# The attention of a diffusion layer in an order written out for all engines, with two sets of ring slots

## The chip, the cores and the metric

One core of a Trainium2 chip runs the whole layer. The metric is the device time of one execution in microseconds (us); the kernel is run several times and the median counts. One more execution is recorded by the hardware profiler, and the rows below are from that one.

The core has five engines that run their own queues in order: PE (TensorE, matrix products into PSUM), VectorE (DVE in the profile), ScalarE (ACT), GpSimd (POOL) and the sync engine (SP), which here only issues DMA transfers. Semaphores carry the waits between them.

## The reference, cut to what matters

```python
def reference(x, c, ctx, c_ctx, w_ada, b_ada, ...):        # 256 latent tokens, 256 context tokens, width 1024
    mod = jnp.split((silu_c @ w_ada[l] + b_ada[l])[:, None, :], 6, axis=-1)      # six rows of 1024
    h = modulate(rms_norm(x, g_mix_pre[l]), mod[0], mod[1])
    y, yc = token_mixing(h, hc, w_in[l], sink[l], g_q_a[l], w_uq[l], g_kv_a[l], w_ukv[l], w_o[l], ...)
    x = x + mod[2] * rms_norm(y, g_mix_post[l])
    h2 = modulate(rms_norm(x, g_ffn_pre[l]), mod[3], mod[4])
    f = moe_ffn(h2, w_router[l], b_router[l], w_gate_up[l], b_gate_up[l], w_down[l], b_down[l])
    return x + mod[5] * rms_norm(f, g_ffn_post[l])

def token_mixing(h, hc, w_in, ...):
    qa, ka, va, cq, ckv, kr = jnp.split(h @ w_in, PROJ_SPLITS, axis=-1)
    out_a = windowed_gqa(qa, ka, va, ka_c, va_c, sink)       # 8 heads, 2 of keys and values, with a sink logit
    qn, qr, kn, vb = mla_project(cq, ckv, g_q_a, w_uq, g_kv_a, w_ukv)   # low rank 384 and 256, norm, up-projection
    out_b = mla_latent(qn, qr, kn, kr, vb, kn_c, kr_c, vb_c)            # 8 heads of 64 + 32
    y = jnp.concatenate([out_a, out_b], axis=-1) @ w_o
```

The mixture of experts takes the best 4 of 32 experts for each token; every expert has 12 MiB of weights (gate and up 8, down 4), so 384 MiB in all, and nearly all of the transferred bytes.

## The kernel before

Everything is float32. The work stands in this order:

1. *Run-up.* The first two rows of the modulation (products of `w_ada` on PE), norm, transposes and the combined input projection `w_in`, each weight split into a high and a low part (`split`, L127) so that three products (`mm3`, L134) give full precision. `stage_a` and `stage_b` apply rope and transpose q and k of the GQA heads; `lowrank` (L354) norms and transposes the MLA latents; `up` (L461) makes the MLA keys `pk`.
2. *Attention.* 16 heads in 8 pairs `u`: 0 to 3 GQA, 4 to 7 MLA. For a pair: `weights(u)` (L636) makes scores with transposed keys on PE, ScalarE takes the exponential into `pT`; the probabilities are summed over keys in `pa` (one head on VectorE, one on GpSimd, L670); `values(u)` (L675) multiplies by v and by ones, then VectorE takes the reciprocal `rz` and writes `oT`; `mix(u)` (L693) multiplies by the output projection into the PSUM tiles `y`. The softmax needs row maxima first: `top_a(j)` for GQA, `top_b(h)` for MLA heads (reductions on VectorE), and `shift(g)` transposes them. The MLA tensors come from `k_up(i)` (L497: copies on ScalarE into `k96`, eight transposes, splits), `q_up(n, t)` (L511: product, copy and rope into `q96`, four transposes, split) and `v_up(i)`.
3. *The other four rows of the modulation* ("ada", chunks 0 to 3) are made beside all this, away from PE. Item i = 4 ch + s is one load of 1 MiB (`ada_load`, L404) and its work (`ada_do`, L415): two halves, each multiplied by a column of silu(c) and summed into `accs[ch]`. A half listed in `ADA_G` goes through ScalarE (product, L422) and GpSimd (sum, L423); the other half is one VectorE instruction (L425). Both write the same sum, so they come one after the other. `column` and `spread1` bring finished rows into the form that the layer needs; `spread0` loads a gain row for it on ScalarE's queue.
4. *Router* (`XSEQ`, L66 and L903), then 32 *experts* (L1094): for each, `G_` (gate and up, matmuls at L972 into `pw`), `T_` (SwiGLU), `D_` (down), `scatter` into `acc`.

Expert weights come in 384 loads of 1 MiB (`load`, L703). Load number n goes to slot `RSEQ[n % 18]`: `d0` to `d2` are the tiles that held the latents and the GQA q and k, `r` a ring slot, `k0 q0 b0 k1 q1 b1` the MLA tensors of head group 0 and 1, `x` four slots in the work memory of the attention, free after the last `values` and `mix`. The ring (`slot`, L79) has R1 = 5 slots of 1 MiB that everything uses: ada items, pieces of `w_in`, `w_ukv`, `w_uq`, the split of v (`v_split`), `w_o` (`load_wo`), gain rows, `scr` and `ar_` in the run-up.

Order: the sync engine always follows the program text, and an issue that waits for its slot holds the ones behind it. In the run-up the other engines are ordered by the compiler's scheduler. From L725 on PE follows the text too; ScalarE, VectorE and GpSimd follow it only from L787, after `mix(6)`. Whatever the order is, it is fixed before the run.

Of the kernel before, what the change touches and what calls it, by code (L numbers as in the profile page):

```python
# [18 lines left out]
P = 128  # L19
# [51 lines left out]
def layer_kernel(ctx, tc, x, cx, cc, wadr, bada, grows, win0, winB, winC, winD, wuqa, wuqb, wukv, wo, wr, wexp, bgu, bgx, bdn, cols, rows, consts, out):  # L71
# [6 lines left out]

    def slot():  # L79
        return ring.tile([P, 2048], F32, name="slot", tag="slot")  # L80

# [112 lines left out]
    def load_ada(i):  # L194
        w = slot().rearrange("p (k c) -> p k c", c=D)
        nc.sync.dma_start(w, wadr[i].rearrange("p (k c) -> p k c", c=D))
        return w
# [7 lines left out]
    scr = slot().rearrange("p (j d) -> p j d", j=2)  # L205
# [19 lines left out]
    def fetch(src, n):  # L225
        w = slot()
        nc.sync.dma_start(w[:, 0:n], src)
        return w
# [61 lines left out]
    ar_ = slot().rearrange("p (j d) -> p j d", j=2)  # L290
# [150 lines left out]
    fkv = fetch(wukv, 1024)  # L441
    fuq = [fetch(wuqa, 1536)]
# [5 lines left out]
    fuq += [fetch(wuqb, 1792)]  # L448
# [48 lines left out]
    def k_up(i):  # L497
        k96 = pqa.tile([P, 8, 96], F32, name="k96", tag="ct", bufs=2)
        S.copy(k96[:, :, 64:96], krt[:, i][:, None].to_broadcast([P, 8, 32]))
        S.copy(k96[:, :, 0:64], pk[i].rearrange("p (h d) -> p h d", h=8))  # L500
        for g in range(2):
            pt = ptp((96, 4, P))
            for j in range(4):
                PE.transpose(pt[:, j], k96[:, g * 4 + j], ident)
            ks = slice(i * P, (i + 1) * P)
            split(kTm[0][g][0:96, :, ks], kTm[1][g][0:96, :, ks], pt)
# [4 lines left out]
    def q_up(n, t):  # L511
        if n == 0:
            q96[t] = pqa.tile([P, 8, 96], F32, name="q96", tag="ct", bufs=2)
# [3 lines left out]
        S.copy(q96[t][:, n * 4:n * 4 + 4, 0:64], pq_[:, :, 0:64])  # L517
        rope(sm, q96[t][:, n * 4:n * 4 + 4, 64:96].rearrange("p h (a d) -> p h a d", a=2),
             pq_[:, :, 64:96].rearrange("p h (a d) -> p h a d", a=2), row[:, t, R_CB:R_CB + 32],
             row[:, t, R_SB:R_SB + 32], 16, 4)  # L520
        pt = ptp((96, 4, P))
        for j in range(4):
            PE.transpose(pt[:, j], q96[t][:, n * 4 + j], ident)
# [23 lines left out]
    def load_wo(i):  # L547
        w = slot()
# [11 lines left out]
    def spread0(ch):  # L560
        gs_[ch] = slot()
        S.dma_start(gs_[ch][:, 0:D], bass.AP(tensor=grows.tensor, offset=grows.offset + (0 if ch == 0 else 1) * D,
# [31 lines left out]
    def top_a(j):  # L594

        for t in range(NT):
            s_ = [pmm((P, 512)) for h in range(2)]
            kb = 3 - t
            for h in range(2):
                PE.matmul(s_[h][:, kb * P:(kb + 1) * P], ident_b, mask_b[:, t * P:(t + 1) * P], start=True, stop=False,  # L600
                          skip_group_check=True)
            for h in range(2):
                PE.matmul(s_[h], qTg[0][HALF[h], t, j], kTg[0][HALF[h]], start=False, stop=True, skip_group_check=True)
            for h in range(2):
                V.tensor_reduce(mxs["a"][:, t, 64 * h + j:64 * h + j + 1], s_[h], axis=AX.X, op=ALU.max)
# [30 lines left out]
    def weights(u):  # L636
# [3 lines left out]
        pa_[u] = [av.tile([P, 2, T], F32, name="pa", bufs=3) for h in range(2)]  # L640
        for g in range(2):
# [26 lines left out]
            for h in range(2):  # L668
                S.activation(pT_[u][h][:, 2 * g:2 * g + 2], st[h], AF.Exp, scale=A_SCALE if a else B_SCALE)  # L669
        for h in range(2):  # L670
# [4 lines left out]
    def values(u):  # L675
        pT, pa = pT_.pop(u), pa_.pop(u)
# [26 lines left out]
    def load(e, js):  # L703
        for j in js:
            q = RSEQ[len(slots) % len(RSEQ)]
            if q == "r":
                w = slot()
# [20 lines left out]
    k_up(1)  # L728
    top_a(1)
    ada(1)  # L730
    k_up(2)
    k_up(3)
    top_a(2)
    top_a(3)
    v_split()
    ada(2)
    for t in range(NT):
        q_up(0, t)
    for i in range(2):
        v_up(i)  # L740
    shift("a")
    clear(1)
    for t in range(NT):
        q_up(1, t)
    for i in range(2, 4):
        v_up(i)
    open_y()
    ada(1)
    load_wo(0)
    for j in range(4):  # L750
        weights(j)
        if j:
            values(j - 1)
        top_b(2 * j)
        top_b(2 * j + 1)
        if j > 1:
            mix(j - 2)
        if j % 2:
            shift(j // 2)
        if j == 0:  # L760
            load_wo(1)
            spread0(0)
        if j == 1:
            column(1)
            spread1(0)
        ada(2)
        if j == 3:
            load(0, range(0, 3))
    for u in range(4, 8):
        weights(u)  # L770
        values(u - 1)
        mix(u - 2)
        if u < 6:
            load_wo(u - 2)
        if u == 4:
            column(2)
            ada(2)
        if u == 5:
            load(0, range(3, 6))
        if u == 6:  # L780
            spread0(3)
            spread1(3)
    values(7)
    mix(6)
    if MANX:
        stM.close()
# [520 lines left out]
```

## Time and profile before

| | us |
|---|---|
| median of 3 runs | 1241.83 |
| lowest, highest | 1241.19, 1244.47 |
| the profiled execution | 1246.29 |
| its span, first to last instruction | 1244.5 |
| PE busy | 1125.8 |
| VectorE, ScalarE, GpSimd busy | 309.8, 241.7, 131.0 |
| bytes read from HBM | 444.6 MB |

The busy times are sums over stages that have different limits. The useful way to read this profile is by stage: how fast DMA runs, and which wait ends last in each.

### The profile page before, as it was taken

The numbers are of one execution on the slowest core, as the hardware profiler recorded it, in microseconds if no ns is written. First come the engines' busy times: TensorE is split into PE (matmuls) and PEld (weight loads), VectorE is DVE, ScalarE is ACT, GpSimd is POOL, SyncE is SP. The second block draws the span as 40 slices with busy tenths as digits, with TensorE's granted clock in tenths as the row PEclk, the third lists the DMA queues.
The fourth block names the chain that finished last, engine by engine and source line by source line (L and its number), as shares of the span: only waits on it lengthen the run. The fifth ranks groups of instructions, "written<-read, shape, count | busy, mean of one in ns | idle before, by whom it ended". The sixth has DMA issues, their size and how long they took to land.

```text
span 1244.5 us, 13660 instructions
## 1 busy us (share of the span) xinstructions
PE 1125.8 (90%) x5455; PEld 485.7 (39%) x5455; DVE 309.8 (25%) x657; ACT 241.7 (19%) x518; POOL 131.0 (11%) x177
## 2 busy tenths in 40 slices
PE   7796758999999999999999999989898989898985
PEld 1694435656334343433323232323232323232321
DVE  3878472335211111111111111111111111111112
ACT  3645220213111111111111111111111111111201
POOL 0414030111000101011010101010101010101000
PEclk9897876999899999999999999999999999999998
DMA  9654150558989999999999999999999999999994
GB/s 366 253 213 172 65 220 1 225 233 320 421 323 421 420 420 420 420 420 419 421 421 420 420 419 421 421 420 421 420 421 421 420 421 420 421 420 421 420 421 197
DMA packets 63195, 446.60 MB, mean 359 GB/s; under 512 B 7284, under 2 KB 7540, under 8 KB 10008
## 3 DMA queue, kind: packets, MB, share of 16 engines
q1 hardware_dynamic: 62648, 444.24, 87.0%
q10 hardware_dynamic: 480, 1.44, 0.4%
q8 instruction: 45, 0.74, 0.2%
q14 instruction: 22, 0.18, 0.0%
HBM read 444.60 MB, written 1.05 MB: 358 GB/s over the span
## 4 chain that ended last, share of the span: by engine, by line
DMA 53%; PE 36%; DVE 7%; issue 2%; ACT 1%; POOL 0%; SPq 0%; POOLq 0%; ACTq 0%; DVEq 0%
DMA slot<-in_wexp 51%; PE pw L972 18%; PE y L696 3%; DMA slot<-in_wadr 2%; PE px L939 2%; PE mm L660 2%; PE acc L1002 1%; PE mm L267 1%; DVE accw L425 1%; PE mm L681 1%; PE pf L985 1%; PE pr L516 1%; PE mm L138 1%; PE mm L139 1%; PE mm L137 1%
## 5 line engine op out<-in xcount | busy, mean ns | idle before, releaser
L972 PE MATMUL pw<-slot,xg 128*64 128x512 f32 x2048 | 468.5, 599 | 19.3 <-DMA slot<-in_wexp 19.3
L972 PE MATMUL pw<-slot,actT 128*64 128x512 f32 x1024 | 242.8, 600 | 28.6 <-DMA slot<-in_wexp 27.1
L972 PEld LDWEIGHTS pw<-slot,xg 128*64 128x64 f32 x2048 | 136.6, 137 | 302.9 <-issue 232.0
L990 DVE TENSOR_TENSOR z<-pf,bg 128x512 f32<-128x512 f32 x64 | 44.3, 692 | 755.5 <-PE pf L985 755.5
L972 PEld LDWEIGHTS pw<-slot,actT 128*64 128x64 f32 x1024 | 68.6, 136 | 179.1 <-issue 101.7
L994 ACT ACTIVATE sg<-z 128x256 f32<-128x256 f32 x64 | 26.7, 417 | 311.9 <-DVE z L992 311.9
L979 ACT COPY gu<-pw 128x512 f32<-128x512 f32 x64 | 37.5, 586 | 230.2 <-PE pw L972 230.2
L939 PEld LDWEIGHTS px<-oh,xt 128*128 128x128 f32 x480 | 57.5, 196 | 23.9 <-issue 23.9
L1002 PE MATMUL acc<-y,ctt 64*128 64x512 f32 x256 | 63.6, 615 | 0.7 <-ACT y L979 0.7
L939 PE MATMUL px<-oh,xt 128*128 128x128 f32 x480 | 63.2, 286 | 0.3 <-DVE cnt L1057 0.3
L951 ACT ACTIVATE xg<-px,vcol 128x128 f32<-128x128 f32 x120 | 45.2, 457 | 92.2 <-PE px L939 92.2
L985 PEld LDWEIGHTS pf<-con,gu 128*128 128x128 f32 x256 | 26.8, 140 | 52.7 <-issue 51.1
L985 PE MATMUL pf<-con,gu 128*128 128x128 f32 x256 | 42.0, 286 | 0.7 <-ACT gu L979 0.7
L979 ACT COPY y<-pw 128x512 f32<-128x512 f32 x32 | 18.8, 587 | 91.1 <-PE pw L972 91.1
L929 POOL TENSOR_SCALAR oh<-con,posm,r 128x64 f32<-128x64 f32 x60 | 33.9, 581 | 2.5 <-DVE posm L869 2.5
L696 PE MATMUL y<-slot,of 128*128 128x512 f32 x64 | 33.7, 678 | 0.0
L996 DVE TENSOR_TENSOR sg<-z,sg 128x256 f32<-128x256 f32 x64 | 27.2, 425 | 18.0 <-ACT sg L994 18.0
L1002 PEld LDWEIGHTS acc<-y,ctt 64*128 64x128 f32 x256 | 22.0, 186 | 21.8 <-issue 18.4
L669 ACT ACTIVATE pT<-mm 128x512 f32<-128x512 f32 x32 | 17.2, 594 | 61.8 <-PE mm L660 58.8
L997 DVE SCALAR_TENSOR_TENSOR actT<-z,sg 128x256 f32<-128x256 f32 x64 | 27.2, 425 | 2.2
L267 PE MATMUL mm<-slot,siluz 128*4 128x512 f32 x40 | 19.4, 635 | 7.4 <-DMA slot<-in_wadr 7.4
L966 ACT COPY ctt<-px 128x256 f32<-128x256 f32 x32 | 12.0, 375 | 61.8 <-PE px L965 61.8
(450 smaller groups left out, 920.4 us busy)
## 6 DMA issues: line engine op xcount, KB each, us to landing
slot<-in_wexp SPq DMA_DIRECT2D x384, 1024.0 KB, 19.9
slot<-in_wadr SPq DMA_DIRECT2D x20, 1024.0 KB, 5.6
ax<-in_wadr SPq DMA_DIRECT2D x4, 1024.0 KB, 4.9
slot<-in_wo SPq DMA_DIRECT2D x4, 1024.0 KB, 7.7
slot<-in_win SPq DMA_DIRECT2D x2, 1024.0 KB, 8.1
slot<-in_winD SPq DMA_DIRECT2D x2, 768.0 KB, 7.3
slot<-in_winB SPq DMA_DIRECT2D x2, 576.0 KB, 5.6
ct<-in_cx SPq DMA_DIRECT2D x2, 512.0 KB, 13.2
```

The costliest lines, as they stand in the source:

```text
L267: PE.matmul(pad[ch][n], siluz[:, 2 * s + k], w[:, k, n * 512:(n + 1) * 512], start=(s == 0 and k == 0), stop=(last and k == 1), skip_group ...
L696: PE.matmul(y[t][n], oT[k][:, t * P:(t + 1) * P], wov[k][:, n * 512:(n + 1) * 512], start=(k == 0), stop=(k == KD - 1), skip_group_check=True)
L929: eng.tensor_scalar(oh[t][:, i], iota[:, 0:CAP], pos_ap(t), r2[t], op0=ALU.is_equal, op1=ALU.mult)
L939: PE.matmul(px[:, k, 0:ne * CAP], xt[t][:, kk * P:(kk + 1) * P], self.oh[t][:, 0:ne].rearrange("p e c -> p (e c)"), start=(k == 0 and t == ...
L951: S.activation(o, i, AF.Identity, scale=vcol[:, 1, kk:kk + 1], bias=vcol[:, 0, kk:kk + 1])
L972: PE.matmul(pt[HALF[h]], lhs(k), wk(k, h), start=(k == 0), stop=(k == KD - 1), skip_group_check=True)
L979: S.copy(y, pt)
L985: PE.transpose(pf[:, b].rearrange("p h c -> p (h c)"), gu[:, b * P:(b + 1) * P], ident)
L990: V.tensor_tensor(z, pf, bias[:, :, :, None].to_broadcast([P, 4, 2, CAP]), op=ALU.add)
L996: V.tensor_tensor(sg, zg, sg, op=ALU.mult)
L997: V.scalar_tensor_tensor(actT[:, 4 * c:4 * c + 4], zl, 1.0, sg, op0=ALU.add, op1=ALU.mult)
L1002: PE.matmul(acc[t][n], ctt[HALF[n], t], y[HALF[n]], start=False, stop=last, skip_group_check=True)
```

## The change

The tags and sizes: the ring is cut into three `slot` tiles and two `wide` ones. Loads of the run-up alternate between them (`any_slot`); `w_ukv`, both `w_uq` pieces and `w_o` take `wide` ones, ada items of the attention and `v_split` the three others. `scr` and `ar_` move to held tiles, the gain rows to the tag `ct`, which `k96` and `q96` use too. `q96` becomes one tile for each half. In the expert loads two `r` become `w`.

The work on engines: chunk 3 of the ada sums also goes half through ScalarE and GpSimd (twelve items instead of eight). The subtraction in `v_split` goes from VectorE to GpSimd. The sums `pa` move from the end of `weights` to the start of `values` (`adds`). In `q_up` rope comes ahead of the copy.

The order: from the first `ada_load` of the attention on, ScalarE, VectorE and GpSimd follow the text as well. `k_up` and `q_up` are cut into a part that computes (`k_mid`, `q_up`) and one that transposes (`k_flip`, `q_flip`), and the text is a list of calls: key transposes among the GQA maxima, then `weights(0)` to `weights(3)` with q and v up-projections between them, the expert loads `d0` to `d2`, then MLA maxima between `mix` calls, and MLA pairs. One ada item at a time stands between them, sixteen in all by `mix(5)`; then five loads of expert 0 and one of expert 1 follow, ahead of `weights(7)`.

```diff
-R1 = 5
+R1 = 3
-RSEQ = ("d0", "d1", "d2", "r", "r", "r", "k0", "q0", "b0", "k1", "q1", "b1", "r", "r", "x", "x", "x", "x")
-ADA_G = {(c, s, k) for c in (1, 2) for s in range(4) for k in range(1)}
+RSEQ = ("d0", "d1", "d2", "r", "r", "r", "k0", "q0", "b0", "k1", "q1", "b1", "w", "w", "x", "x", "x", "x")
+ADA_G = {(c, s, 0) for c in (1, 2, 3) for s in range(4)}
+    def wide():
+        return ring.tile([P, 2048], F32, name="slot", tag="wide", bufs=2)
+    def any_slot():
+        turn[0] += 1
+        return wide() if turn[0] % 5 in (3, 4) else slot()
-    scr = slot().rearrange("p (j d) -> p j d", j=2)
+    scr = held(1).rearrange("p (j d) -> p j d", j=2)
-    ar_ = slot().rearrange("p (j d) -> p j d", j=2)
+    ar_ = held(2).rearrange("p (j d) -> p j d", j=2)
-    fkv = fetch(wukv, 1024)
-    fuq = [fetch(wuqa, 1536)]
+    fkv = fetch(wukv, 1024, wide)
+    fuq = [fetch(wuqa, 1536, wide)]
-    fuq += [fetch(wuqb, 1792)]
+    fuq += [fetch(wuqb, 1792, wide)]
-        split(r[:, 0:1024], r[:, 1024:2048], fuq[1][:, 768:1792])
+        split(r[:, 0:1024], r[:, 1024:2048], fuq[1][:, 768:1792], eng=G)
-        w = slot()
+        w = wide()
         nc.sync.dma_start(w, wo[i])
-        gs_[ch] = slot()
+        gs_[ch] = pqa.tile([P, D], F32, name="gs", tag="ct", bufs=2)
     def values(u):
+        adds(u)
         pT, pa = pT_.pop(u), pa_.pop(u)
+    stM.close()
+    stM.enter_context(tc.manual_schedule(engines={SP, *[getattr(mybir.EngineType, e_) for e_ in MANX]}))
     ada_load()
     ada_load()
-    stM.close()
-    stM.enter_context(tc.manual_schedule(engines={SP, mybir.EngineType.PE}))
-    k_up(0)
-    top_a(0)
...
     v_split()
+    k_mid(2)
+    k_mid(3)
+    for i in (2, 3):
+        top_a(i - 2, 0)
+        k_flip(i)
+        top_a(i - 2, 1)
...
+    v_up(0)
+    q_up(0, 0)
+    v_up(1)
     shift("a")
     clear(1)
+    weights(0)
+    q_flip(0, 0)
+    q_up(0, 1)
+    v_up(2)
+    ada(1)
+    weights(1)
+    v_up(3)
+    q_flip(0, 1)
+    q_up(1, 0)
+    values(0)
+    ada(1)
+    weights(2)
+    q_flip(1, 0)
+    q_up(1, 1)
+    values(1)
+    ada(1)
+    load_wo(0)
+    weights(3)
+    q_flip(1, 1)
+    values(2)
+    load_wo(1)
+    load(0, range(0, 3))
     open_y()
     ada(1)
+    top_b(0)
+    mix(0)
+    spread0(0)
+    top_b(1)
+    top_b(2)
+    ada(1)
+    column(1)
+    top_b(3)
+    mix(1)
+    values(3)
+    ada(1)
+    load_wo(2)
+    top_b(4)
+    shift(0)
+    mix(2)
+    ada(1)
+    weights(4)
+    spread1(0)
+    top_b(5)
+    mix(3)
+    ada(1)
+    load_wo(3)
+    weights(5)
+    top_b(6)
+    values(4)
+    column(2)
+    top_b(7)
+    mix(4)
+    ada(2)
+    shift(1)
+    spread0(3)
+    values(5)
+    ada(1)
+    weights(6)
+    ada(1)
+    mix(5)
+    load(0, range(3, 8))
+    load(1, range(0, 1))
+    weights(7)
+    values(6)
+    spread1(3)
+    mix(6)
     values(7)
     mix(KD - 1)
-    load(0, range(6, 8))
-    load(1, range(0, 4))
+    load(1, range(1, 4))
     load(0, range(8, 12))
```

## Rows read from the trace of the kernel before

**Rows 1.** The page's 40 slices: busy share of the DMA engines, in tenths.

```profile
DMA  9654150558989999999999999999999999999994
```

**Rows 2.** Chain that ended last, whole span: start us, length us, what.

```profile
299.88 10.45 PE pw L972 x48
...
588.02 19.86 DMA slot<-in_wexp
...
1209.06 19.50 DMA slot<-in_wexp
```

**Rows 3.** Table of stages: busy us (instructions) by engine, granted clock, DMA share, GB/s.

```profile
155.00:186.00 31.00, 17.45 (x118) 11.50 (x116) 21.56 (x22) 7.58 (x12) 10.15 (x6) 0.76 0.61 228
186.00:217.00 31.00, 25.71 (x130) 17.30 (x132) 9.89 (x17) 2.54 (x5) 1.99 (x2) 0.64 0.00 1
249.00:280.00 31.00, 29.69 (x158) 18.01 (x157) 10.65 (x14) 4.34 (x8) 4.00 (x4) 1.00 0.58 231
300.00:588.00 288.00, 285.57 (x1364) 108.73 (x1361) 48.89 (x133) 48.39 (x110) 23.01 (x40) 0.98 0.98 405
588.00:1228.00 640.00, 591.84 (x2764) 210.19 (x2764) 87.58 (x215) 92.43 (x208) 43.76 (x76) 1.00 1.01 419
```

**Rows 4.** Timeline of the sync engine: start us, length us, line, operation, count.

```profile
268.16 1.28 SPq L713 DMA_DIRECT2D slot<-in_wexp  x3
...
284.35 17.76 SPq L713 DMA_DIRECT2D slot<-in_wexp  x6
```

**Rows 5.** Chain that ended last, end of the run-up and first key transposes.

```profile
94.26 1.21 DVE accw L425
...
110.06 0.61 DVE cn L359
...
117.71 1.89 PE tp L504 x8
```

**Rows 6.** The same chain in the attention: PE pieces at full clock.

```profile
138.47 1.95 PE pr L516 x6
...
216.09 1.62 PE mm L660 x22
...
230.17 3.79 PE mm L660 x32
233.97 1.88 PE mm L681 x16
...
236.71 3.63 PE y L696 x8
...
261.59 1.72 PE mm L570 x4
```

**Rows 7.** The same chain: waits, ada work, and PE pieces at half clock.

```profile
151.51 6.42 DMA slot<-in_wadr
157.95 1.16 ACT slot L422
159.18 2.37 POOL accw L423
...
172.57 5.28 DMA slot<-in_wadr
...
196.50 3.57 PE mm L570 x4
...
209.86 6.24 PE y L696 x8
...
265.68 0.60 ACT pT L669
```

**Rows 8.** Timeline of VectorE: the low part of the v split.

```profile
96.57 2.50 DVE L129 TENSOR_TENSOR slot<-slot 128x1024 fp32r<-128x1024 f32 x1 [0.92 <-ACT slot L128]
```

**Rows 9.** Line 672, VectorE's part: ns min/median/max, first and last start us.

```profile
L672 DVE TENSOR_TENSOR pa<-pT x8: 684/814/2330, 165.0 to 271.4; 128x512 f32<-128x512 f32 x8
```

**Rows 10.** Waits of the sync engine: us in total, times, longest.

```profile
SPq L713 <- PE mm L666: 40.0, 1, 40.0
```

More of the change, by code (lines that the diff above doesn't have):

```diff
@@ L194, in load_ada @@
     def load_ada(i):
-        w = slot().rearrange("p (k c) -> p k c", c=D)
+        w = any_slot().rearrange("p (k c) -> p k c", c=D)
         nc.sync.dma_start(w, wadr[i].rearrange("p (k c) -> p k c", c=D))
@@ L223, in norm_t, with fetch @@
             S.copy(xraw[2 * w + g][:, :, j], p_)
-    def fetch(src, n):
-        w = slot()
+    def fetch(src, n, get=any_slot):
+        w = get()
         nc.sync.dma_start(w[:, 0:n], src)
@@ L495, in layer_kernel, with k_mid, k_flip @@
                           mask_b[64 * c:64 * c + 64].rearrange("p (t k) -> p t k", t=NT))
[L497 to L500, printed above, removed]
+    k96 = {}
+    def k_mid(i):
+        k96[i] = pqa.tile([P, 8, 96], F32, name="k96", tag="ct", bufs=2)
+        S.copy(k96[i][:, :, 0:64], pk[i].rearrange("p (h d) -> p h d", h=8))
+        S.copy(k96[i][:, :, 64:96], krt[:, i][:, None].to_broadcast([P, 8, 32]))
+    def k_flip(i):
         for g in range(2):
@@ L511, in q_up @@
     def q_up(n, t):
-        if n == 0:
-            q96[t] = pqa.tile([P, 8, 96], F32, name="q96", tag="ct", bufs=2)
+        q96[n, t] = pqa.tile([P, 4, 96], F32, name="q96", tag="ct", bufs=2)
         pq_ = prow((P, 4, 96))
@@ L547, in load_wo @@
     def load_wo(i):
-        w = slot()
+        w = wide()
         nc.sync.dma_start(w, wo[i])
@@ L592, in layer_kernel, with top_a @@
     ess = {}
[L594 to L605, printed above, removed]
+    def top_a(j, t):
+        s_ = [pmm((P, 512)) for h in range(2)]
+        kb = 3 - t
+        for h in range(2):
+            PE.matmul(s_[h][:, kb * P:(kb + 1) * P], ident_b, mask_b[:, t * P:(t + 1) * P], start=True, stop=False,
+                      skip_group_check=True)
+        for h in range(2):
+            PE.matmul(s_[h], qTg[0][HALF[h], t, j], kTg[0][HALF[h]], start=False, stop=True, skip_group_check=True)
+        for h in range(2):
+            V.tensor_reduce(mxs["a"][:, t, 64 * h + j:64 * h + j + 1], s_[h], axis=AX.X, op=ALU.max)
     def top_b(h):
@@ L639, in weights @@
         pT_[u] = [av.tile([P, 4, T], F32, name="pT", bufs=4) for h in range(2)]
-        pa_[u] = [av.tile([P, 2, T], F32, name="pa", bufs=3) for h in range(2)]
         for g in range(2):
@@ L669, in weights, with adds @@
                 S.activation(pT_[u][h][:, 2 * g:2 * g + 2], st[h], AF.Exp, scale=A_SCALE if a else B_SCALE)
+    def adds(u):
+        pa_[u] = [av.tile([P, 2, T], F32, name="pa", bufs=3) for h in range(2)]
         for h in range(2):
@@ L705, in load @@
             q = RSEQ[len(slots) % len(RSEQ)]
-            if q == "r":
-                w = slot()
+            if q in "rw":
+                w = slot() if q == "r" else wide()
             elif q == "x":
@@ L741, in layer_kernel @@
+    k_mid(2)
[4 more added lines that the diff above has]
+        top_a(i - 2, 1)
+    k_mid(0)
+    k_mid(1)
+    for i in (0, 1):
+        top_a(i + 2, 0)
+        k_flip(i)
+        top_a(i + 2, 1)
+    v_up(0)
+    q_up(0, 0)
+    v_up(1)
     shift("a")
     clear(1)
[L743 to L746, printed above, removed]
+    weights(0)
[5 more added lines that the diff above has]
+    v_up(3)
@@ L747, in layer_kernel @@
+    q_flip(0, 1)
[13 more added lines that the diff above has]
+    load(0, range(0, 3))
     open_y()
     ada(1)
[L749 to L782, printed above, removed]
+    top_b(0)
[11 more added lines that the diff above has]
+    top_b(4)
@@ L783, in layer_kernel @@
+    shift(0)
[21 more added lines that the diff above has]
+    mix(5)
+    assert ada_n[0] == 16 and not ada_q
+    load(0, range(3, 8))
[4 more added lines that the diff above has]
+    mix(6)
     values(7)
-    mix(6)
-    if MANX:
-        stM.close()
-        stM.enter_context(tc.manual_schedule(engines={SP, *[getattr(mybir.EngineType, e_) for e_ in MANX]}))
```

24 lines of the change are left out of this document (7 added, 17 removed).

## The prediction, made before the changed kernel was run

> **What bounds the kernel now.** I read the page's slices first, then the chain that ended last, then the queue of the sync engine (SP), and only then the attention. The slices, 31 us each, say that the kernel has two parts: ten slices with low and middle digits of DMA, and then nines up to the end [rows 1]. In the chain that ended last, matmuls of the experts start at 299.88, and from 588.02 the chain is nothing but landings of expert weights of 19.9 us each, thirty-two of them, the last at 1209.06 [rows 2]. The table of stages confirms it: 419 GB/s from 588 on, with PE busy 592 of 640 us; between 300 and 588 it is the other way round, PE 285.6 of 288 us and DMA 405 GB/s [rows 3]. So the end is a stream of expert weights, 384 loads of 1 MiB. At 419 GB/s one takes 1.0486 MB / 419 GB/s = 2.50 us. The stream cannot be shortened by this change; it can be shifted.
>
> What fixes where the stream lies? There are 18 slots for expert weights. The sync queue's issues show the last of the first 18 going out from 284.35 on, when the last `mix` frees the work memory, and then a pause; the row that begins there ends 17.76 us later with the next issue, 0.33 us long, at 301.8, when the first expert matmuls (299.88) give back a slot [rows 2, 4]. Five or six loads at 2.50 fill that pause, so DMA and PE are in step there: the eighteen slots have just been filled when the first is reused. From then on the two parts of the kernel run the same way whenever they begin: PE-paced until the backlog is used up, DMA-paced afterwards. An earlier first expert matmul moves the whole rest by the same amount, as long as the eighteen loads are there by then too. Between the last `mix` (it ends at 284.3) and 299.88 lies the router, 15.6 us, which the change does not touch. So the question is how much earlier `mix(7)` ends.
>
> The attention begins for PE with the key transposes, after the last low-rank norm (110.06 + 0.61 [rows 5]) and its own 0.7 us of transposes, at 111.4, and takes 284.3 - 111.4 = 172.9 us. In two windows of 31 us PE is busy 17.5 and 25.7 us, at a granted clock of 0.76 and 0.64; from 249 on it is 29.7 of 31 at 1.00 [rows 3]. The first half has room, the last third has almost none.
>
> **How much PE work there is.** Prices are lengths of pieces of the chain, which do not overlap, at the 2.4 GHz level of the clock [rows 5, 6]. Key transposes 4 x 1.89 = 7.6; q up-projections 4 x 1.95 = 7.8; scores of a GQA pair 4 x 2.3 = 9.2 (22 matmuls take 1.62, the rest and the masks 0.7); scores of an MLA pair 4 x 3.79 = 15.2; values 8 x 1.88 = 15.0; output projection 8 x 3.63 = 29.0; spread products 2 x 1.72 = 3.4. The smaller kinds, read in the same view, make some 32: row maxima 12.6, v up-projections 5.6, sums and sinks of `values` 5.1, columns and router bias 5.2, q transposes 2.5, shifts 0.9. Together 119, taken as 120 us. The other 53 of the 172.9 are waits and half clock. The waits are named in the chain: 6.42 and 5.28 us for ada weights to land, then 1.16 on ScalarE and 2.37 on GpSimd, before VectorE comes to the maxima that PE needs; the half clock is in pieces like 3.57 for a spread product that takes 1.72 later, and 6.24 for a `mix` that takes 3.63 [rows 6, 7]. These two alone cost 4.5 us.
>
> **Part by part.**
>
> *Ring sets, and `scr` and `ar_` in held tiles.* The first ada loads get five slots, not four. DMA's first digit is a nine already [rows 1], so under 3 us can come of it; I take 1, which the rounding swallows. Against it: `wukv` and both `wuq` loads now share two wide slots with one piece of `w_in` each, and SP issues in order, so each waits until the piece before it in its slot is split, 10 to 20 us later than now, with the third and fourth ada loads of the right-hand pool behind them. They are needed for the splits at the end of the run-up and, for q and v, some 15 us into the attention; that distance is the cover, and without it each would cost its landing of 5 us.
>
> *Ada items 4 to 7 leave the run-up.* Before, VectorE does their sums among the low-rank norms that the first key transposes follow: three of some 1.21, and the v split of 2.50 [rows 5, 8], which goes to GpSimd: 6.1 us. GpSimd's own sums of 2.37 stand ahead of the norm's power there. Against that, two late items of chunk 0 come into this stretch, some 2.4 us more than now. Bounds: 0 (another chain, such as the late ada loads, takes over) to 8 (all of it and the powers). I take 5, since these rows lie on the chain itself. PE's attention begins at 106.4.
>
> *The written order.* It places all attention instructions of ScalarE, VectorE and GpSimd by hand. q and v up-projections, which before stand by themselves with holes for copies and rope, go between GQA scores; MLA maxima go between output products. The work stays 120. What it adds, from rows:
> Entry and mask copies on VectorE: 2. PE waits for exponentials between the two halves of a score: 0.60 [rows 7], 8 times at most, I take 3.
> The probability sums now sit at the head of `values`, both engines starting together. Over its eight sums VectorE took 0.68 at least and 2.33 us at most [rows 9]; the longest was the one that met a GpSimd ada sum. PE has 1.88 of matmuls to cover it; 8 x 0.6, I take 5; bounds 0 and 8 x 1.6 = 13. The Trainium skill, SBUF — State Buffer, section Who interferes with whom, gives this as a lock: a VectorE instruction with two SBUF inputs blocks while a GpSimd one reads SBUF, and issue order decides which of the two waits. The row agrees, and it speaks against giving GpSimd more; what it could do in full is a rival below.
> The ada items: twelve, and now all of one form, ScalarE product 1.16, GpSimd sum 2.37, VectorE sum 1.21 [rows 5, 7], each waiting for the one before. The VectorE instruction is in line, so maxima, reciprocals and the `pa` sums queue behind it for up to 1.16 + 2.37 = 3.5 us, and PE behind those. For chunk 3 four VectorE sums of 1.21 are saved, four GpSimd ones added. Bounds: 0, and 12 x 3.5 = 42. PE holds other work at eight of the twelve places (a score, a `values` or a `mix` of 2 to 4 us); at four it does not (the router bias after `column(1)`, both MLA shifts, the second-last `values`). 4 x 3.5, less what PE finishes meanwhile: 12. Landing is not the wait: two items are loaded ahead, and the queue has no other traffic then.
> Clock: in the trace PE fell to the 1.2 GHz level after waits such as those for ada weights. I count four holes that stay (the four places above); one piece of `mix` size at half speed costs 2.6 [rows 6, 7]. 4 x 2.3 = 9; bounds 0 and the last rival below.
> Sum: 120 + 2 + 3 + 5 + 12 + 9 = 151.
>
> *Moved loads.* `d0` to `d2` come out of the queue after GQA scores that end some 60 us earlier; SP waited 40.0 us at one point for those [rows 10]. The six loads `r r r k0 q0 b0` now stand behind the last ada load, where two or three slots are still held by ada items 13 to 15. Then k1 q1 b1 wait for `weights(7)`, and six for the last `mix`, as before (three issues at 268.16, others from 284.35 [rows 4]). Fifteen loads need 37.5 us. From the last ada sums to the router's end lie `weights(7)`, two `values`, three `mix` and 15.6 us of router, some 40 us: it just fits. `spread0` takes a q96 tile in place of a ring slot, queues on ScalarE behind what is written ahead of it, and has several products of cover before its use.
>
> **Sum.** `mix(7)` ends at 106.4 + 151 = 257.4 in place of 284.3: 26.9 us earlier, 27 with rounding. The profiled execution took 1246.29 us, 1244.5 of span and 1.8 around it, and lies 4.5 above the median 1241.83. Its twin would be 1219; from the median, 1241.8 - 27 = 1215 us.
>
> **Rivals.**
> *The order hides nearly everything.* No VectorE stall reaches PE: 151 - 12 - 9 + some 5 = 135, start at 106.4: 241.4, 43 earlier, 1199 us. For it: in the stretch from 249, PE ran so already, with the other engines a third busy or less [rows 3]. Against: the serial ada triple.
> *The ada triples come late one after another.* Three slots, one held by v until the fourth up-projection, give each next load only after the sum before it: 5 us of landing and 1.16 + 2.37 + 1.21 of work [rows 5, 7], 12 x 9.7 = 116 us of a chain that must end before `spread1(3)`. If 15 us more of it show, 166 us and 12 earlier: 1230 us.
> *DMA is late.* If the fifteen loads start d after the point above, the stream moves by d less than PE. Some 10 us of DMA idling between 300 and 588 (405 against 419 GB/s [rows 3]) absorb the first part. With d = 15, 5 us of gain are lost: 1220 us, inside the main case's range.
> *The clock stays low (slower).* Many short matmuls with small waits between them keep PE on the 1.2 GHz level, as in the window from 186 [rows 3]. A share f of the 120 us then costs 120 f more. Break-even is 106.4 + 142 + 120 f = 284.3, f = 0.30. At f = 0.6 the attention takes 214 us, ends at 320: 36 later, 1278 us. For it: 0.64 granted in 186 to 217. Against: that window began with a VectorE wait and products of one column, and the last third, as dense as the new order is meant to be, is at 1.00 [rows 3].
> *GpSimd holds VectorE up, and the gain is gone (no change).* A hit costs 2.33 - 0.68 = 1.65 us [rows 9]. Twelve ada sums and eight `pa` pairs are 20 places; if every one meets a VectorE instruction with two SBUF operands and PE waits behind each, that is 33 us, 28 more than I counted: 179 us, `mix(7)` at 285.4, 1243 us. For it: the order puts the `pa` pair side by side on purpose, and ada sums next to it. Against: maxima read PSUM, and most VectorE work of this part is of that kind.
>
> **Chances.** Main 0.52 (with late DMA 0.06 within it), all hidden 0.19, late ada triples 0.14, GpSimd hold-ups 0.06, low clock 0.09. About 0.3% (3.7 us) is what a measurement of this kernel can tell from no change. Faster: 0.52 + 0.19 + 0.14 = 0.85; same 0.06; slower 0.09. The range leaves out the slow rival, the hold-ups and the far end of late ada work: 1197 (hidden, and the start 2 us better) to 1233.
>
> **What the profile would show.** Right: first `px`/`pw` matmuls of the experts near 273; three windows of 31 us from 110 on with PE over 25 busy and clock over 0.85; SP's 40 us wait gone; waits of VectorE `accw`/`vpost` sums for GpSimd as the longest ones of the attention, with PE idle behind maxima and shifts; 419 GB/s to the end. Wrong, if PE idle appears before key transposes (start), if the granted clock is under 0.7 over 100 us (clock), if DMA has a hole between the last `mix` and the first expert (loads), or if the stretch before 111 grew.

## The result, and the profile after

Before, the kernel took 1243.15 us (median; 1241.19 to 1244.79); changed, it takes **1220.57 us** (1219.89 to 1221.49): 0.9819 of the time before, 95% interval 0.9801 to 0.9838, 22.6 us less. The profiled execution of the changed kernel took 1221.49 us with a span of 1219.7, 24.8 us shorter than the span before. The execution profiled before, 1246.29 us, lies 3.1 above its median, so a difference between the two traces comes out somewhat larger than one between the medians.

The page's slices of the granted clock and of the DMA engines' busy share, in tenths (30.5 us each), answer to [rows 1]:

```profile
PEclk9999989899899999999999999999999999999998
DMA  9641374499899999999999999999999999999994
```

The eights and nines of DMA begin in the ninth slice, before in the tenth. After that the kernel is the stream of expert weights it was. PE's timeline (start us, length us, line, operation, count; in brackets the idle time before it and its releaser) gives the three points from which the sum was made: key transposes, last `mix`, first expert matmuls.

```profile
106.54 2.23 PE L517 MATMUL tp<-con,k 128*96 128x128 f32 x8
...
252.43 5.40 PE L711 MATMUL y<-slot,of 128*128 128x512 f32 x8 [2.34 <-DVE of L706]
...
273.38 10.52 PE L1010 MATMUL pw<-slot,xg 128*64 128x512 f32 x48
```

The attention lasts 257.8 - 106.5 = 151.3 us, before 172.9. The first expert matmul of 273.4 answers to 299.88 in [rows 2], which PE's timeline has at 299.81: 26.4 us earlier. The table of stages (busy us and instructions of PE, PE's weight loads, VectorE, ScalarE, GpSimd; granted clock, DMA share, GB/s) has the attention in one row, and then the first stretches of the stream, each laid 26.4 us earlier than before:

```profile
107.00:258.00 151.00, 129.81 (x733) 81.53 (x732) 87.32 (x121) 47.46 (x85) 53.23 (x32) 0.91 0.49 190
...
273.40:323.60 50.20, 47.76 (x209) 19.68 (x210) 12.37 (x44) 9.13 (x22) 1.19 (x2) 0.90 0.88 358
```

The same stretch of before:

```profile
299.80:350.00 50.20, 47.77 (x209) 19.68 (x210) 12.39 (x44) 8.88 (x21) 1.19 (x2) 0.90 0.87 354
```

PE works 47.76 against 47.77 us with the same count: the stream is the same one, begun earlier. The attention of before, in the same view:

```profile
111.00:284.00 173.00, 140.41 (x737) 89.19 (x737) 81.33 (x123) 38.63 (x74) 27.56 (x24) 0.81 0.39 148
```

So the gain has three parts: the attention begins 4.9 us earlier; PE is idle 151 - 129.8 = 21.2 us in place of 32.6; and nearly the same number of matmuls takes 129.8 us in place of 140.4, at a granted clock of 0.91 in place of 0.81. What ended PE's waits there (waits of PE from 106 to 258: us in total, times, longest):

```profile
PE mm L638 <- DVE mx L635: 7.1, 2, 4.1
PE mm L698 <- DVE pa L687: 4.8, 3, 2.6
...
PE y L711 <- DVE of L706: 2.7, 2, 2.3
PE mm L672 <- DVE of L706: 2.5, 3, 1.1
...
PE mm L598 <- DVE accw L595: 1.6, 1, 1.6
```

All of them are waits for VectorE: for the negated maxima in `shift` (L635), the probability sums (L687), the normalized output (L706), the router's column (L595). VectorE also waits for GpSimd's ada sums (its waits, same stretch), 18.0 us in five waits:

```profile
DVE accw L434 <- POOL accw L432: 10.0, 3, 4.6
...
DVE vpost L434 <- POOL vpost L432: 8.0, 2, 5.5
```

Most of these 18.0 us do not come before a long wait of PE: of PE's two waits for L635, the one of 3.00 us before `shift(1)` has a wait of VectorE for GpSimd (2.51 us) right ahead of it, the one of 4.12 before `shift(0)` has none.

The chain that ended last shows the longest of PE's waits from inside, the one before `shift(0)`:

```profile
183.50 1.77 DVE rz L704
...
185.63 1.27 DVE accw L434
186.91 1.20 DVE mx L625 x2
188.11 0.09 DVE mx L635
...
188.24 0.50 PE mm L638 x2
188.74 5.07 PE y L711 x8
```

PE had nothing left from 184.1 on; VectorE, in its written order, still did a reciprocal, an ada sum and the maxima of a further head before the negation that PE wanted, an instruction of 0.16 us (0.09 of it in the chain). The `mix` behind the wait then ran 5.07 us, not the 3.60 of the same eight matmuls elsewhere in this trace.

### The profile page after: what moved, and what is told of

Read it like the earlier page. It is cut to its first block, busy times and chain, and to the rows that moved or that the text cites. A ratio compares the mean times of both kernels' runs of the same rounds, so it can differ in the third digit from the quotient of the medians.

```text
span 1219.7 us, 13658 instructions
## 1 busy us (share of the span) xinstructions
PE 1112.8 (91%) x5455; PEld 476.3 (39%) x5455; DVE 307.5 (25%) x652; ACT 245.3 (20%) x522; POOL 149.1 (12%) x182
## 4 chain that ended last, share of the span: by engine, by line
DMA 68%; PE 22%; DVE 7%; issue 2%; ACT 1%; POOL 1%; SPq 0%; POOLq 0%; ACTq 0%; DVEq 0%
DMA slot<-in_wexp 65%; PE pw L1010 8%; PE y L711 2%; DMA slot<-in_wadr 2%; PE mm L276 2%; PE mm L672 1%; PE px L977 1%; DMA ax<-in_wadr 1%; PE acc L1040 1%; DVE accw L434 1%; DVE rz L704 1%; PE mm L696 1%; PE mm L146 1%; PE mm L147 1%; PE mm L148 1%
## 5 line engine op out<-in xcount | busy, mean ns | idle before, releaser
L1010 PEld LDWEIGHTS pw<-slot,xg 128*64 128x64 f32 x2048 | 136.5, 137 | 303.5 <-issue 232.3
L711 PE MATMUL y<-slot,of 128*128 128x512 f32 x64 | 36.4, 722 | 2.7 <-DVE of L706 2.7
L1017 ACT COPY y<-pw 128x512 f32<-128x512 f32 x32 | 18.7, 586 | 91.4 <-PE pw L1010 91.4
L124 POOL TENSOR_TENSOR rstd<-rstd,mh 128x1 f32<-128x1 f32 x14 | 11.2, 799 | 126.1 <-DVE rstd L121 110.3
L432 POOL TENSOR_TENSOR accw<-accw,slot 128x1024 f32<-128x1024 f32 x8 | 19.3, 2419 | 44.0 <-ACT slot L431 38.3
```

Source lines behind the costliest of these rows:

```text
L711: PE.matmul(y[t][n], oT[k][:, t * P:(t + 1) * P], wov[k][:, n * 512:(n + 1) * 512], start=(k == 0), stop=(k == KD - 1), skip_group_check=True)
L1010: PE.matmul(pt[HALF[h]], lhs(k), wk(k, h), start=(k == 0), stop=(k == KD - 1), skip_group_check=True)
L1017: S.copy(y, pt)
```

## The experiments

Thirteen kernels beside the one before, their medians and what their traces show (us). The last column is span less first expert matmul, so what the stream of experts takes. The columns after the median come from the profiled execution, which in two rows lies far from the median: before (1246.29) and "one ring" (1224.62); their times are read from the median. The kernel of the last row turned out to be the changed kernel once more: its median is 0.7 us lower, its key transposes begin 1.2 us later and its attention is 1.7 us shorter. Differences of that size say nothing here.

| kernel | median (range) | key transposes begin | last `mix` ends | first expert matmul | rest |
|---|---|---|---|---|---|
| before | 1243.15 (1241.19 to 1244.79) | 111.4 | 284.3 | 299.8 | 944.7 |
| changed | 1220.57 (1219.89 to 1221.49) | 106.5 | 257.8 | 273.4 | 946.3 |
| only PE's order written | 1210.64 (1208.81 to 1212.52) | 111.2 | 247.7 | 263.1 | 946.0 |
| the same, chunk 3 on VectorE | 1213.40 (1212.28 to 1214.23) | 112.3 | 249.5 | 265.0 | 946.0 |
| one ring | 1219.57 (1217.82 to 1224.62) | 107.3 | 261.9 | 277.4 | 945.4 |
| chunk 3 on VectorE | 1216.98 (1214.46 to 1217.29) | 108.4 | 253.6 | 269.5 | 946.0 |
| all ada sums on VectorE | 1216.13 (1213.65 to 1216.31) | 108.0 | 254.1 | 269.6 | 944.5 |
| twelve ada items not summed | 1202.07 (1201.63 to 1206.35) | 106.9 | 239.1 | 254.7 | 945.4 |
| VectorE's half first | 1222.66 (1221.03 to 1226.85) | 107.8 | 260.4 | 276.0 | 945.3 |
| probability sums early | 1224.96 (1224.35 to 1226.75) | 107.5 | 261.0 | 276.5 | 946.1 |
| both of these | 1227.29 (1225.39 to 1229.07) | 108.1 | 264.0 | 279.6 | 945.2 |
| ada loads ahead | 1219.55 (1219.17 to 1220.48) | 107.1 | 257.2 | 272.7 | 945.0 |
| five ada items in the run-up | 1223.76 (1220.26 to 1224.77) | 113.5 | 261.2 | 276.7 | 945.5 |
| expert loads later in the text | 1219.91 (1218.97 to 1221.77) | 107.7 | 257.3 | 272.9 | 945.4 |

The last column settles the frame of the sum for all fourteen: first expert matmuls between 254.7 and 299.8, and behind them 944.5 to 946.3 us. What the attention gains or loses is carried to the end whole.

**What the ada work costs.** The sums of items 4 to 15 left out, loads kept:

```diff
-            for k in range(2):
+            for k in range(0 if ch else 2):
```

> All sums of ada items 4 to 15 (chunks 1 to 3) are left out, their loads stay; so the gates and the router's bias lack these terms. Theory of the prediction (ada work costs 12 us of stalls and some of the 9 us of half clock): 1201 to 1209 us, and the last mix ends 12 to 20 us earlier than 257.8. Rival (the order hides the ada work already; PE waits for the maxima and probability sums by themselves): 1217 to 1221 us.

Measured: 1202.07 us, 18.5 us less than the changed kernel, and the last `mix` ends 18.7 us earlier. The theory holds. Its table of stages, from key transposes to the last `mix`:

```profile
107.00:239.00 132.00, 120.01 (x732) 77.67 (x730) 65.30 (x113) 35.17 (x72) 19.82 (x20) 0.96 0.52 208
```

PE is busy 120.0 us, not 129.8, for the same matmuls, and idle 12.0, not 21.2. So the ada sums cost 9.2 us of idle PE and 9.8 us by which the same work takes longer, at a granted clock of 0.91 in place of 0.96. PE's wait for the probability sums falls with them, from 4.8 to 1.3 us, and the wait before `shift(1)` is gone. Before `shift(0)` 2.93 of 4.12 us stay, and before the router's column 0.72 of 1.57: there VectorE has other work in its line.

**How much of that is GpSimd's share.** First chunk 3 alone, then all chunks, wholly on VectorE:

```diff
-ADA_G = {(c, s, 0) for c in (1, 2, 3) for s in range(4)}
+ADA_G = {(c, s, 0) for c in (1, 2) for s in range(4)}
```

> Chunk 3 of the ada sums wholly on VectorE, as before the change: four chains of product 1.16, GpSimd sum 2.37, VectorE sum 1.21 become two VectorE sums of 1.2 each. Theory of the prediction (VectorE waiting in line for GpSimd is what the ada work costs): 1216 to 1220 us, some 0 to 4 us faster. Rival (the relief of VectorE by four sums of 1.21 is worth having): 1222 to 1226 us.

Measured: 1216.98 us, 3.6 us less than changed (2.9 less than its repeat) and in the range of the theory. The 4.12 us before `shift(0)` stay. The wait before `shift(1)`, 3.00 us in the changed kernel, is 1.82 here, the one for the sums of `values(4)` 0.39 in place of 1.86.

```diff
-ADA_G = {(c, s, 0) for c in (1, 2, 3) for s in range(4)}
+ADA_G = set()
```

> The changed kernel with all ada sums on VectorE: twelve chains of product 1.16, GpSimd sum 2.37, VectorE sum 1.21 become twelve pairs of VectorE sums of 1.21. Theory (GpSimd's sum costs more by waits and by holding VectorE than it relieves; four items gave 3.6 us): 1208 to 1214 us. Rival (in the first half of the attention VectorE is the next bound, and eight more sums of 1.21 show there): 1217 to 1224 us.

Measured: 1216.13 us, between the two expectations: the eight items of chunks 1 and 2 give no more than 0.9 us beyond chunk 3. PE's waits (106 to 258) say why:

```profile
PE mm L638 <- DVE mx L635: 8.8, 2, 5.4
...
PE mm L598 <- DVE accw L595: 2.9, 1, 2.9
...
PE mm L698 <- DVE pa L687: 1.3, 2, 0.9
```

The wait for probability sums falls from 4.8 to 1.3 us, but the waits before `shift` and for the router's column grow, from 7.1 to 8.8 and from 1.6 to 2.9: here VectorE's own sums stand in its line. So giving chunk 3 to GpSimd, as the change did, cost some 3 us in this order; for chunks 1 and 2 it hardly matters which engine has them.

**Is it the wait in line?** VectorE's half of each item first, so that it waits for a GpSimd sum long done:

```diff
-            for k in range(2):
+            for k in (1, 0):
```

> In each ada item VectorE's own half comes first and GpSimd's half after it, so that VectorE waits for a GpSimd sum of the item before, some 10 us old, and not for one that has just begun; the work is the same. Theory (the wait in line for GpSimd, 18.0 us in five waits of the changed kernel, is what the ada work mostly costs): 1208 to 1215 us, and VectorE's waits for GpSimd's sums under 4 us in all. Rival (the sums themselves and the hold-up of two engines in SBUF cost it, whatever the order): 1217 to 1222 us.

Measured: 1222.66 us, none of the gain. VectorE's five waits of 18.0 us shrink to two of 5.0, but PE's waits, in sum, do not shrink. The time comes back as longer instructions. VectorE's timeline, and then GpSimd's:

```profile
170.56 2.57 DVE L595 TENSOR_TENSOR accw<-wrs,vcol 128x256 f32<-128x256 f32 x1
...
190.15 2.27 DVE L635 TENSOR_SCALAR mx<-mx 128x8 f32<-128x8 f32 x1
```

```profile
170.51 2.34 POOL L432 TENSOR_TENSOR accw<-accw,slot 128x1024 f32<-128x1024 f32 x1 [2.42 <-DVE vcol L594]
...
189.17 2.34 POOL L432 TENSOR_TENSOR accw<-accw,slot 128x1024 f32<-128x1024 f32 x1 [14.12 <-issue]
191.45 0.95 POOL L417 MEMSET vpost<- 128x1024 f32 x1
```

The product of L595 takes 0.42 us in the changed kernel and 2.57 here, beside a GpSimd sum that began 0.05 us before it; the negation of L635, 0.16 us for eight columns there, takes 2.27 here. These 2.11 us are just what PE's wait before `shift(0)` grows by, from 4.12 to 6.23. The wait before `shift(1)`, where VectorE had waited for GpSimd, does shrink, from 3.00 to 1.50. So the wait in line was there, but whether VectorE waits for the sum by a semaphore or is held by it, PE waits, and the rival holds for the time.

**Where the probability sums stand.** Back to the end of their score:

```diff
     def weights(u):
 ...
+        adds(u)
 ...
     def values(u):
-        adds(u)
```

> The probability sums go back to the end of their score, one product earlier than in the changed kernel; everything else as there. Theory (at the head of the values product they are late: PE waits 4.8 us for them, and 1.88-us products behind run at half clock): 1213 to 1218 us and PE's wait for the sums near 0. Rival (early sums make VectorE wait in line for the exponentials, and maxima and reciprocals queue behind): 1219 to 1225 us, with VectorE waiting for ScalarE's pT.

Measured: 1224.96 us, 4.4 slower. The rival holds: VectorE waits 11.8 us for exponentials in front of the sums, and what stands behind in its line comes late, the maxima among it:

```profile
PE mm L638 <- DVE mx L635: 5.6, 2, 4.1
PE mm L672 <- ACT pT L681: 5.3, 2, 2.7
PE y L712 <- DVE of L707: 5.3, 3, 2.3
PE mm L624 <- DVE mx L625: 3.2, 2, 1.8
```

PE no longer waits for the sums at all; it waits 5.3 us for exponentials and 3.2 in front of the products for maxima, where the changed kernel has no such waits. Both edits together:

> VectorE's half first in each ada item and probability sums at the end of their score, together. Theory (two causes that add up): the sum of the two gains, 1202 to 1211 us, near the kernel without ada sums at 1202. Rival (both remove the same idle time, a VectorE that comes late to the next thing PE needs): no more than 2 us better than the better of the two alone.

Measured: 1227.29 us, no gain of either kind: 6.7 us slower than the changed kernel, about the sum of 2.1 and 4.4. The 2.1 lies within the spread of these runs, so that the two add up is not shown.

**Is the written order of the other engines worth having?** PE's order as changed, ScalarE, VectorE and GpSimd left to the scheduler until the last `mix`:

```diff
-    stM.enter_context(tc.manual_schedule(engines={SP, *[getattr(mybir.EngineType, e_) for e_ in MANX]}))
+    stM.enter_context(tc.manual_schedule(engines={SP, mybir.EngineType.PE}))
 ...
     values(7)
+    stM.close()
+    stM.enter_context(tc.manual_schedule(engines={SP, *[getattr(mybir.EngineType, e_) for e_ in MANX]}))
```

> PE's order as in the changed kernel, but ScalarE, VectorE and GpSimd placed by the scheduler until the last mix, as before the change. Theory 1 (the gain is PE's order: up-projections between GQA heads, maxima between output products; the other engines follow in any sensible order): 1217 to 1226 us. Rival (the written places of the ada sums and the probability sums on VectorE and GpSimd carry a good part of the 22.6 us): 1228 to 1243 us, with PE idle behind VectorE in the attention well above the some 19 us of the changed kernel.

Measured: **1210.64 us**, 0.9741 of before (0.9711 to 0.9771): 9.9 us below the changed kernel and faster than either expectation. So the gain of the change does not need the order written for the three other engines, which takes some 10 us of it back. It does not need the earlier start either: this kernel begins its attention at 111.2, as before. What is left as its cause is, above all, PE's order, together with the order of the loads that stands in the same text; the one without the other was not tried, nor PE's order alone in the kernel before. Its stage (111 to 248), and PE's timeline around `shift(0)`:

```profile
111.00:248.00 137.00, 125.02 (x736) 79.94 (x736) 77.06 (x121) 43.11 (x80) 36.16 (x28) 0.92 0.49 192
```

```profile
180.23 0.74 PE L624 MATMUL mm<-kTm,qTm 96*128 96x512 f32 x2
180.80 0.38 PE L638 MATMUL mm<-con,mx 128*128 128x128 f32 x2
181.02 3.60 PE L711 MATMUL y<-slot,of 128*128 128x512 f32 x8
```

PE idles 12.0 us, and the 4.12 us before `shift(0)` are gone: the scheduler put the negation right behind the last maximum that it needs, and the ada sum after it. VectorE's timeline there:

```profile
172.49 1.29 DVE L625 TENSOR_REDUCE mx<-mm 128x1 f32<-128x512 f32 x2 [0.35 <-PE mm L624]
173.82 0.17 DVE L635 TENSOR_SCALAR mx<-mx 128x8 f32<-128x8 f32 x1
176.66 1.28 DVE L434 SCALAR_TENSOR_TENSOR accw<-slot,silu,accw 128x1024 f32<-128x1024 f32 x1 [2.67 <-POOL accw L432]
```

In the written order the negation stands behind `values(3)`, an ada sum and `top_b(4)`, whose head belongs to the other group. The second probability add (ns min/median/max), in the changed kernel and then here:

```profile
L687 POOL TENSOR_TENSOR pa<-pa x8: 787/1592/1659, 137.0 to 240.9; 128x256 f32<-128x256 f32 x8
L687 DVE TENSOR_TENSOR pa<-pa x8: 425/426/2546, 140.0 to 245.8; 128x256 f32<-128x256 f32 x8
```

```profile
L687 POOL TENSOR_TENSOR pa<-pa x8: 727/730/1071, 136.1 to 227.5; 128x256 f32<-128x256 f32 x8
L687 DVE TENSOR_TENSOR pa<-pa x8: 355/360/829, 137.1 to 230.4; 128x256 f32<-128x256 f32 x8
```

What lengthens them in the changed kernel is mostly an ada sum on the other engine. GpSimd's add runs beside one of VectorE's seven times of eight, and then takes 1.58 to 1.66 us. VectorE's add takes 2.45 and 2.55 us where it runs beside an ada sum of GpSimd, 1.40 once beside GpSimd's probability adds, and 0.42 or 0.43 otherwise. As the scheduler places them, the medians are 0.73 and 0.36 us and nothing is over 1.1.

The scheduler also put five ada items (4 to 8) into the run-up, the last sum at 113.4; the change had moved these out. Is that the gain? Those five there, all else as written:

```diff
+    stM.enter_context(tc.manual_schedule(engines={SP, mybir.EngineType.PE}))
     ada_load()
     ada_load()
+    ada(5)
+    stM.close()
+    stM.enter_context(tc.manual_schedule(engines={SP, *[getattr(mybir.EngineType, e_) for e_ in MANX]}))
 ...
-    ada(1)
```

(the last line stands for five such calls in the attention)

> Five ada items (4 to 8) are summed in the run-up, where the scheduler finds room, as it did by itself in the run with only PE's order written; in the attention the written order of all engines stays, less these five. Theory A (where the ada sums lie is the 10 us by which that run was faster): 1208 to 1214 us, with key transposes up to 5 us after 106.5. Theory B (the 10 us are the scheduler's own order of maxima, reciprocals and probability sums in the attention): 1219 to 1226 us, the later start only costs.

Measured: 1223.76 us: theory B. PE's timeline:

```profile
113.53 2.27 PE L517 MATMUL tp<-con,k 128*96 128x128 f32 x8
...
192.89 0.69 PE L638 MATMUL mm<-con,mx 128*128 128x128 f32 x2 [4.12 <-DVE mx L635]
```

The start comes 7.0 us later and the attention is only 3.7 shorter (147.6); the wait before `shift(0)` is still 4.12. So the place of the ada items is not the 10 us, and what remains is the scheduler's order inside the attention. Which single one of its moves carries how much was not tried apart. Last, chunk 3 on VectorE in that version:

```diff
-ADA_G = {(c, s, 0) for c in (1, 2, 3) for s in range(4)}
+ADA_G = {(c, s, 0) for c in (1, 2) for s in range(4)}
```

> Only PE's order written, and chunk 3 of the ada sums wholly on VectorE. Theory (the gains of the two add up: 10 and 3.6 us): 1205 to 1209 us. Rival (the scheduler already puts the sums of chunk 3 where PE does not wait for them): 1209 to 1213 us.

Measured: 1213.40 us, 0.4 above the range of the rival: no gain. Where the scheduler places GpSimd's sums of chunk 3, taking them away from GpSimd saves nothing.

**Rings and loads.** One ring of five slots:

```diff
-R1 = 3
+R1 = 5
 ...
     def wide():
-        return ring.tile([P, 2048], F32, name="slot", tag="wide", bufs=2)
+        return slot()
```

> The changed kernel with one ring of five slots in place of three and two. Theory (the two sets are worth nothing by themselves; the sum gave them 0 to 1 us): 1219 to 1223 us, and the loads of wukv, wuqa, wuqb and of the third and fourth ada piece go out some 10 us earlier, or not, without moving the end by more than 2 us. Rival (one ring puts a short-lived ada load behind a slot that v or an output weight holds, so ada pieces come late): 1226 to 1236 us, and waits of ScalarE's ada product for DMA.

Measured: 1219.57 us: the theory holds, the two sets are worth nothing by themselves. The third and fourth ada piece go out at 70.4 and 80.5 in place of 83.9 and 94.2, and the key transposes begin no earlier (107.3). Next, the run-up's late ada pieces ahead of the up-projection weights in the sync queue:

```diff
     ada_load(p1)
-    fkv = fetch(wukv, 1024, wide)
-    fuq = [fetch(wuqa, 1536, wide)]
 ...
     ada_load(p1)
+    fkv = fetch(wukv, 1024, wide)
+    fuq = [fetch(wuqa, 1536, wide)]
     fuq += [fetch(wuqb, 1792, wide)]
```

> The third and fourth ada pieces of the run-up are issued ahead of wukv and both wuq pieces in the sync queue, not behind them. Theory (the late pieces, landing at 90.8 and 98.9, hold VectorE ahead of the last low-rank norms): key transposes start 2 to 4 us before 106.5, 1216 to 1219 us. Rival (the norm, its power on GpSimd and the projections set the start anyway): within 1 us of the changed kernel. Third case (wukv now lands too late for its split): start later, 1222 us or more.

Measured: 1219.55 us, start 107.1: the rival. The chain of the changed kernel runs through the landings of these two pieces (6.87 us from 83.93, 4.69 from 94.19); with the pieces earlier it runs through products of PE up to 101.8 and then the last norm, and ends at the same time. And the six expert loads, moved behind the last `mix` in the text:

```diff
-    load(0, range(3, 8))
-    load(1, range(0, 1))
 ...
     mix(KD - 1)
+    load(0, range(3, 8))
+    load(1, range(0, 1))
```

> The six expert loads that stand behind the last ada load go behind the last mix, where nine more wait anyway. From 257.8 fifteen loads of 2.50 us last to 295, 20 us beyond the first reuse of a slot at 275.4. Theory of the prediction (the stream moves, and DMA idling of some 8 to 10 us between 275 and 588 absorbs the first part): 10 to 12 us slower than the changed kernel, 1229 to 1234 us, with the first expert matmul still near 273. Rival (the loads are hidden behind PE until the backlog is used up): 1219 to 1223 us. Other rival (nothing is absorbed): 1239 us or more.

Measured: 1219.91 us, which says nothing on the question. Between the two places stands no instruction of the sync engine, so the order on every engine is unchanged: the run repeats the changed kernel (0.7 us apart). A late DMA was therefore not tried; the constant last column of the table is what speaks against it.

## Why the prediction was right, step by step

*Start of the attention.* 106.4 foreseen, 106.5 measured. That the moved items are the reason is borne out from the other side: with five ada items in the run-up again it begins at 111.2 to 113.5. The share of the v split, 2.50 us of the 6.1, was not tried apart. Two limits lie close together here: the landings of the late ada pieces, which the prediction names as its lower bound, and PE's own products behind them.

*Work of 120 us.* 120.0 us of busy PE in the kernel without ada sums; but part of that agreement is luck. Its granted clock is 0.96, so some 0.04 x 132 / 0.5 = 10.6 us lay at the 1.2 GHz level. If PE was busy in them, half, 5.3 us, is loss, and the work at 2.4 GHz is some 115 us, an estimate.

*Waits and clock.* Foreseen 2 + 3 + 5 + 12 = 22 us of idle PE and 9 of half clock; measured 21.2 idle. The half clock, reckoned as above from 0.91 over 151 us, is some 13.6 us (an estimate too): the work was put some 5 us too high and the half clock some 5 too low, and the two errors cancel. Inside the 22 the shares were not all right. The 2 for the entry are 1.9, but for maxima, not for copies. Waits for exponentials, put at 3, do not appear among PE's waits. The probability sums, put at 5, are 4.8, and for another reason: the two engines do not start together, and 4.4 of the 4.8 are two waits for a VectorE add that an ada sum of GpSimd held (2.45 and 2.55 us in place of 0.42). For the ada sums 12 us were put at four places: PE waits 1.57 + 4.12 + 3.00 = 8.7 us at three of these, 3.7 of which stay without any ada sum, and not at all at the fourth. In all the ada sums cost 9.2. The rest are waits for the output of `values` in front of products that follow at once (5.2), which I had no term for. The mechanism for the 12 was half wrong: I priced the wait in line, and the run with VectorE's half first shows that without most of that wait the time is no better, since GpSimd's sum holds the instruction that PE needs. So the size of the sum is right, and its split in part by luck.

*Landing is not the wait.* Half right. "No other traffic" was wrong: from 147.6 on two output weights and three expert pieces go out in front of ada loads, and the chain runs through a landing of 12.97 us, against 5.28 in [rows 7]:

```profile
155.54 12.97 DMA slot<-in_wadr
```

But PE does not wait for it. That load is item 9, and the sum ahead of the router's column is item 8, loaded at 147.2; VectorE's timeline has it behind maxima, not behind a landing:

```profile
167.30 2.49 DVE L625 TENSOR_REDUCE mx<-mm 128x1 f32<-128x512 f32 x4 [1.33 <-PE mm L624]
169.70 1.28 DVE L434 SCALAR_TENSOR_TENSOR accw<-slot,silu,accw 128x1024 f32<-128x1024 f32 x1
...
171.09 0.42 DVE L595 TENSOR_TENSOR accw<-wrs,vcol 128x256 f32<-128x256 f32 x1
```

Here, too, it is the line: the column's two short instructions stand behind an ada sum of 1.28 us that they don't need, and PE waits 1.57 us; 0.72 where that sum is left out.

*End of the attention and the stream.* `mix(7)` 257.4 foreseen, 257.8 measured; first expert matmul 273, measured 273.4. The 40.0 us of [rows 10] are gone. Another wait, which I had not foreseen, has taken their length in the same queue: 40.9 us for the slot that v holds, by its releaser a v up-projection. The ada load behind it goes out at 135.5, and the expert loads still came in time.

*From the profile to the median.* Here lies the error of 5.6 us. The twin of the profiled execution was to take 1219; it took 1221.5: 0.6 us less came at the first expert matmul than rounded up, and the stream took 946.3 in place of 944.7. The larger part is the step after that: I took the median 4.5 us below the profiled execution, as before; in the changed kernel it lies 0.9 below. The execution profiled before was a long one of its kind. Twenty further executions of that kernel lie between 1241.4 us, at a granted clock of 0.967, and 1247.7 at 0.958; the profiled one had 0.958. Its extra length goes with the lower clock, and only part of it came back in the changed kernel.

*The rivals.* The order that hides everything (stage of 135, 1199 us) did not come with this order, but it was within reach: with only PE's order written the stage is 136.5 us, at a start 5 us later. The clock did not stay low: 0.91 granted over the attention, and the slow rival needed 0.30 of the work at half speed; 13.6 of 115 us is 0.12. GpSimd's hold-ups are real, and the two long ones (2.45 and 2.55 against 0.42 us) reach PE, 4.4 us, far from the 33 of the rival. The ada triples did not become one chain of loads and sums: VectorE waited 18.0 us for them, PE 9.2 at most.

## What to carry to other kernels

Write the order of the engine that bounds the stage, and ask of each other engine whether its order must be written too: in one written line a 0.16-us instruction that the bound engine waits for stands behind work that nobody wants yet. Put an instruction on a helper engine where its last input is ready, not where its consumer stands in the text, and not ahead of that input either: in the run with early probability sums VectorE waited 11.8 us for exponentials. Price a move of sums to GpSimd by what PE waits for, not by VectorE's busy time; here GpSimd's sums lengthened VectorE's instructions, and moving four of them cost some 3 us.

## What the runs showed of the hardware

In the run with VectorE's half first, a VectorE instruction of one SBUF operand and eight columns took 2.27 us in place of 0.16 while GpSimd ran a sum of 2.34 us and then, 0.95 us long, a memset: it ended with the memset, 192.4, not with the sum. In the changed kernel the same instruction took 0.69 us beside GpSimd's second probability add, and ended with it (223.0). I had expected such hold-ups of instructions with two SBUF operands only. The Trainium skill, SBUF — State Buffer, section Who interferes with whom, counts `tensor_scalar` among the operations that can contend with GpSimd for a shared pair of ports, which the one that issues first has for its whole instruction. These rows agree, with GpSimd first.

The hold goes both ways and is not rare: GpSimd's short add took 1.59 us by the median in the changed kernel, beside VectorE's ada sums, and 0.73 in the scheduler's order, where only one of the eight runs beside such a sum (0.92). Of 18.0 us of semaphore waits 13 could be removed without a gain, because the same sums then lengthened VectorE's instructions.
